# Layer 1's gate stored ready-made, its norm bias moved into the gate step, and the final norm done in one product, in a one-core hybrid decoder trunk

## The chip, the cores and the metric

The kernel is one program on 1 core of one Trainium2 chip. The metric is the device time of one execution in microseconds (us), as the median of the runs; lower is better. Next to it stands one profiled execution, whose trace gives the rows below. Engines are named as the profile names them: PE (TensorE; PEld is its weight load), DVE (VectorE), ACT (ScalarE), POOL (GpSimd), SP (SyncE, which here only issues transfers). ACT and POOL issue some transfers too.

## What is computed

A trunk of two residual layers on 2048 tokens of width 1024, all in float32. Cut to what matters here:

```
# layer 0: retention heads (A) and stick-breaking attention (B), each gated
mixed = concat([o_a * silu(ga), o_b * silu(gb)]);  h = h + mixed @ w_out
h = h + sigmoid(h @ ple_gate) * (p @ ple_proj)          # after every layer

# layer 1: RWKV-7 mixing; r, k, v, g are four projections of the normed h
y = head_norm(recurrence(r, w, k, v, kk, a)) * lnx_g + lnx_b
bonus = sum(r * k * r_k) * v                              # per head
h = h + ((y + bonus) * silu(g)) @ w_out
h = h + sigmoid(h @ ple_gate) * (p @ ple_proj)
out = h * rsqrt(mean(h * h) + eps) * final_gain           # the final norm
```

## The kernel before

Tokens go in two halves of 1024 (`w` = 0, 1), each in two blocks of 512 (`TB`); channels lie on the 128 partitions, in eight blocks (`NB`). Each float32 matrix product is made of three products of a high and a low part (`mm3`, L239 to L241), and `split` (L199 on ACT, L200 on DVE or POOL) makes these parts. The stages in their order:

- half 0: retention and stick-breaking attention, then `tail(0, 0)` (output projection, per-layer embedding), then `l1_proj` (layer 1's projections and the preparation of the recurrence);
- half 1: the same attention, then **the first merge**: the recurrence of layer 1 for half 0 (`recur`, 16 chunks of 64 tokens) runs beside the layer-0 tail of half 1 (`tail_lean`); then `l1_proj` for half 1;
- **the second merge**: the recurrence for half 1 beside three blocks of layer 1's tail (`tail_lean` with l = 1: both blocks of half 0, the first of half 1);
- the final tail: `tail(1, 1)` for the last block, and beside it `finish`, which writes the normed output of the three earlier blocks.

`merge` weaves two generators by planned costs, and a scheduler then sets each engine's order from its own planned timeline. On the chip every engine works its list strictly in that order. Tiles come from pools with a fixed number of buffers, and whoever wants a buffer waits until its last user is done.

The places that the change touches:

- `g_proj` (L1231) projects the gate in groups of two channel blocks. `to_dram` (L1105) empties each of the four accumulators of a group: ACT copies it into a tile `ev` (two buffers, L1108) and ACT issues the store (L1109).
- `gated` (L858) loads a block of the recurrence's result (`stage`) and the gate (`g`), and makes stage·g·sigmoid(g): DVE L866, ACT L867, DVE L868. The final tail has its own form: ACT Silu L713, DVE L714.
- in `block`, the new residual is `o` (DVE L941, two buffers); ACT squares it (L946), for l = 1 DVE multiplies it by the final gain (L949), and SP stores it (L950). The final tail does that on ACT (L779).
- `post` (L1589) norms a chunk: POOL multiplies the value tile `vt` by the bonus (L1603) and `y` by the gain (L1604), DVE adds the bias to `vt` (L1605) and `vt` to `y` (L1607). Gain, bias and bonus are loaded by SP at the head of each recurrence (L1647, L1648).

Of the kernel before, what the change touches and what calls it, by code (L numbers as in the profile page):

```python
# [9 lines left out]
F32 = mybir.dt.float32  # L10
# [3 lines left out]
AF = mybir.ActivationFunctionType  # L14
# [58 lines left out]
C_N = C_HX + 4 * P  # L73


V_G0, V_G1, V_GF, V_MU, V_W0, V_A0, V_KK, V_KA, V_RK, V_GN = 0, 1, 2, 3, 9, 10, 11, 12, 13, 14
V_N = 15


def constants():  # L80
# [54 lines left out]
class Trunk:  # L135
# [44 lines left out]
    def load_vectors(self):  # L180
        nc = self.nc
        v = self.cst.tile([P, V_N * NB], F32, name="vec")
        nc.scalar.dma_start(v, self.i["vec"])
        self.vec = v

        self.omu = self.cst.tile([P, 6 * NB], F32, name="omu")
        nc.vector.tensor_scalar(self.omu, v[:, V_MU * NB : (V_MU + 6) * NB], -1.0, 1.0, op0=ALU.mult, op1=ALU.add)
        self.oka, self.hka = [self.cst.tile([P, NB], F32, name=n) for n in ("oka", "hka")]
        ka = v[:, V_KA * NB : (V_KA + 1) * NB]
        nc.vector.tensor_scalar(self.oka, ka, -0.5, 1.0, op0=ALU.mult, op1=ALU.add)  # L190
        nc.vector.tensor_scalar_mul(self.hka, ka, 0.5)

    def col(self, which, b):
        return self.vec[:, which * NB + b : which * NB + b + 1]
# [491 lines left out]
    def tail(self, l, w, mixed, gates, resid, side=None, ts=range(NTB)):  # L686
# [3 lines left out]
        with ExitStack() as es:  # L690
# [13 lines left out]
            for t in ts:  # L704
                for d in range(NB):
                    sl = slice(t * TB, (t + 1) * TB)
                    gated = gates(d, sl) is not None
                    m = sm.tile([P, TB], F32, tag="m" if gated or d % 2 else "g", name=self.u("m"), bufs=3 if gated or d % 2 else 2)
                    nc.sync.dma_start(m, mixed(d, sl))
                    if gated:  # L710
                        g = sm.tile([P, TB], F32, tag="g", name=self.u("g"))
                        nc.sync.dma_start(g, gates(d, sl))
                        nc.scalar.activation(g, g, AF.Silu)  # L713
                        nc.vector.tensor_tensor(m, m, g, op=ALU.mult)  # L714
                    self.split(m, mx[d][0][:, tok(t)], mx[d][1][:, tok(t)], nc.vector if (d * NTB + t) % 3 < 2 else nc.gpsimd)
            hs = [tuple(hp.tile([P, n], F32R, tag="hp", name=self.u("hp")) for _ in range(2)) for _ in range(NB)]

# [34 lines left out]
            def ple_evac(ob):  # L752
                wq = wqs[ob]

                def evac(t, ps):
                    sl = slice(t * TB, (t + 1) * TB)
                    g = sm.tile([P, TB], F32, tag="g", name=self.u("g"))
                    nc.scalar.activation(g, ps, AF.Sigmoid)
                    q = pp.tile([P, TB], F32, tag="pp", name=self.u("pp"))
                    for d in range(2):  # L760
                        self.mm3(
                            q, (wq[0][:, d], wq[1][:, d]), (pT[d][0][:, tok(t)], pT[d][1][:, tok(t)]), d == 0, d == 1
                        )
                    nc.vector.tensor_tensor(g, g, q, op=ALU.mult)
                    o = sb.tile([P, TB], F32, tag="o", name=self.u("o"))
                    nc.gpsimd.tensor_tensor(
                        o, hs[ob][0][:, tok(t)].bitcast(F32), hs[ob][1][:, tok(t)].bitcast(F32), op=ALU.add
                    )
                    nc.vector.tensor_tensor(o, o, g, op=ALU.add)
                    if ob == 0:  # L770
                        nc.scalar.activation(self.ssacc[:, sl], o, AF.Square)
                    else:
                        nc.scalar.activation(g, o, AF.Square)
                        eng = nc.vector if ob == NB - 1 else nc.gpsimd
                        eng.tensor_tensor(self.ssacc[:, sl], self.ssacc[:, sl], g, op=ALU.add)
                    if l == 0:
                        nc.sync.dma_start(h1[ob][:, sl], o)
                    else:
                        nc.scalar.activation(h1[ob], o, AF.Copy, scale=self.col(V_GF, ob))  # L779

                return evac

# [10 lines left out]
            for t in ts:  # L793
                rbp = self.rows_of(rs[:, (t - ts[0]) * 4 : (t - ts[0]) * 4 + 4], pt)
                for ob in range(NB):
                    o = sb.tile([P, TB], F32, tag="fo", name=self.u("fo"), bufs=8)
                    nc.vector.tensor_tensor(o, rbp, h1[ob][:, tok(t)], op=ALU.mult)
                    (nc.scalar if ob % 2 else nc.sync).dma_start(self.out_at(w, ob, t), o)

    def out_at(self, w, ob, t):  # L800
# [11 lines left out]
    def finish(self, w, h, rs, ts, sb, pt):  # L812
# [11 lines left out]
        for n, (t, ob) in enumerate(units):  # L824
# [2 lines left out]
            if ob == 0:  # L827
                rbp = self.rows_of(rs[:, t * 4 : t * 4 + 4], pt)
            o = sb.tile([P, TB], F32, tag="o", name=self.u("fo"))
            nc.vector.tensor_tensor(o, rbp, xs.pop(0), op=ALU.mult)  # L830
            nc.sync.dma_start(self.out_at(w, ob, t), o)
            yield

    def tail_lean(self, es, parts):
# [23 lines left out]
        def gated(blk, d, tags="g"):  # L858
# [4 lines left out]
            if gates(d, tok(b)) is not None:  # L863
                g = T(tags[d % len(tags)], 2)
                nc.sync.dma_start(g, gates(d, tok(b)))
                nc.vector.tensor_tensor(m, m, g, op=ALU.mult)  # L866
                nc.scalar.activation(g, g, AF.Sigmoid)  # L867
                nc.vector.tensor_tensor(m, m, g, op=ALU.mult)  # L868
            return m

        def spread(staged):
# [8 lines left out]
        def block(blk, staged, following):  # L880
# [33 lines left out]
            for ob in range(NB):  # L914
# [30 lines left out]
                else:  # L945
                    nc.scalar.activation(g, o, AF.Square)  # L946
                    nc.gpsimd.tensor_tensor(self.ssacc[:, sl], self.ssacc[:, sl], g, op=ALU.add)
                if l == 1:
                    nc.vector.tensor_scalar_mul(o, o, self.col(V_GF, ob))  # L949
                nc.sync.dma_start(h1[:, ob, sl], o)  # L950
                yield
            return ahead
# [42 lines left out]
    def l1_proj(self, w, h1):  # L995
# [10 lines left out]
        with ExitStack() as es:  # L1006
# [207 lines left out]
            def v_proj():  # L1214
                xs = mix(2)
                for nh in range(2):
# [12 lines left out]

                    yield from self.proj_N(ws, xs, evac, pj)  # L1230

            def g_proj():
                yield from self.proj_pairs(load(3), mix(3), lambda ob: to_dram(d_g[ob]), pj)

            bnp = pst.tile([P, TB], F32, tag="pt", name=self.u("bnp"))

# [101 lines left out]
    def recur(self, w, es, lean=False, early=0):  # L1338
# [20 lines left out]
        lnx = []  # L1359
        for nm in ("rwkv_lnx_gain", "rwkv_lnx_bias"):  # L1360
            t = fin.tile([P, NB, C], F32, name=self.u("lnx"), bufs=1)
            lnx.append((t, i[nm][0].rearrange("(o s c) -> s o c", s=2, c=C)))
# [225 lines left out]
        def post(s):  # L1588
# [12 lines left out]
            nc.gpsimd.tensor_tensor(y, y, bc(rs), op=ALU.mult)  # L1601
            yield
            nc.gpsimd.tensor_tensor(vt, vt, bc(bonus[:, s]), op=ALU.mult)  # L1603
            nc.gpsimd.tensor_tensor(y, y, lnx[0][0], op=ALU.mult)  # L1604
            nc.vector.tensor_tensor(vt, vt, lnx[1][0], op=ALU.add)  # L1605
            yield
            nc.vector.tensor_tensor(y, y, vt, op=ALU.add)  # L1607
            yield
# [13 lines left out]
        def main():  # L1622
# [19 lines left out]
                yield PRE[1]  # L1642
            for _ in inv(0):
                yield PRE[2]
            for par in range(2):
                for t, src in lnx:
                    nc.sync.dma_start(t[half(par)], src[par].unsqueeze(0).to_broadcast([C, NB, C]))  # L1647
                nc.sync.dma_start(bonus[half(par)], self.d_b[par].rearrange("(c t) o -> t c o", t=C))  # L1648
            b = None
            for s in range(NCH):  # L1650
                self.ready = max(0, s - 1) * C
# [119 lines left out]
def chain(makers):  # L1771
# [18 lines left out]

_INS = [
    "x", "ple_proj", "ple_gate", "even_w_in", "even_w_out", "odd_w_in", "odd_w_out", "rwkv_w1", "rwkv_w2",
    "rwkv_a1", "rwkv_a2", "rwkv_lnx_gain", "rwkv_lnx_bias",
]


def vectors(inputs):
# [3 lines left out]
    for v, x in (  # L1801
# [5 lines left out]
        (V_KK, a("rwkv_k_k", 0)),  # L1807
        (V_KA, a("rwkv_k_a", 0)),
        (V_RK, a("rwkv_r_k", 0)),
    ):  # L1810
        rows[v : v + len(x)] = x
    rows[V_GN, :RH] = np.asarray(inputs["ret_gn_gain"])[0].reshape(RH, P)
# [28 lines left out]
```

## Time and profile before

| | |
|---|---|
| median of 3 runs | 3716.74 us (3715.48 to 3717.23) |
| profiled execution: its own time | 3711.4 us |
| profiled execution: span of the trace | 3709.6 us |
| busy: PE / DVE / ACT / POOL | 91% / 54% / 37% / 26% of the span |
| mean granted PE clock | 0.939 of full speed |

The busy shares are means over stages with different limits. PE's is near the full span, but it holds stretches at a lower granted clock and stretches with gaps. What a change is worth is read from the stage in which it lies, and there from who is waited for.

### The profile page before, as it was taken

How to read it: one execution, taken by the hardware profiler on the slowest of the kernel's cores; microseconds unless marked ns; L12 is line 12 of the kernel's file. 1: busy time of each engine (PE TensorE's matmuls, PEld its weight loads, DVE VectorE, ACT ScalarE, POOL GpSimd, SP SyncE). 2: the span in 40 equal slices, each digit the busy share in tenths (PEclk: the TensorE clock that was granted, in tenths of full speed). 3: DMA queues.
4: the chain of work that ended last, by engine and by line, in shares of the span. 5: the costliest groups of instructions: out<-in, count | busy, mean ns of one | idle time of the engine just before them, and what ended most of it. 6: DMA issues, size and time to landing. Idle time of an engine off the chain costs nothing.

```text
span 3709.6 us, 65403 instructions
## 1 busy us (share of the span) xinstructions
PE 3383.3 (91%) x25640; PEld 2694.0 (73%) x25640; DVE 1991.4 (54%) x3959; ACT 1375.3 (37%) x2671; POOL 971.0 (26%) x1019
## 2 busy tenths in 40 slices
PE   7999999899999999999879998699988698978968
PEld 6888878787666788888767776587656577767756
DVE  3435552452665333567856666641574477566543
ACT  4333442354564222445523333343453143223222
POOL 3345554300000222556512222200000243222322
PEclk9999999899999999999989998699999788979979
DMA  7259765655688216537367655333676777656485
GB/s 263 96 171 271 218 195 177 216 164 182 201 266 288 99 67 194 175 101 148 68 203 210 194 177 144 104 121 138 200 249 178 186 222 211 186 144 183 158 281 197
DMA packets 570788, 671.94 MB, mean 181 GB/s; under 512 B 215408, under 2 KB 416368, under 8 KB 539504
## 3 DMA queue, kind: packets, MB, share of 16 engines
q1 hardware_dynamic: 495072, 578.41, 50.2%
q0 software_dynamic: 40576, 33.56, 4.4%
q10 hardware_dynamic: 34832, 55.78, 4.1%
q8 instruction: 203, 3.33, 0.4%
q14 instruction: 105, 0.86, 0.1%
HBM read 419.50 MB, written 248.12 MB: 180 GB/s over the span
## 4 chain that ended last, share of the span: by engine, by line
PE 71%; DMA 10%; DVE 9%; ACT 3%; SPq 3%; issue 3%; POOL 1%; DVEq 0%; ACTq 0%; POOLq 0%
PE pj L239 17%; PE pj L240 17%; PE pj L241 17%; PE g L1396 2%; PE tp L654 1%; DMA nb<-nad 1%; DVE wb L1450 1%; DVE prd L1444 1%; PE lora L1266 1%; SPq L1429 1%; PE u L1516 1%; PE x L1538 1%; DMA xr<-ar 1%; PE z L625 1%; PE ot L240 1%
## 5 line engine op out<-in xcount | busy, mean ns | idle before, releaser
L239 PE MATMUL pj<-act,w 128*128 128x512 f32 x1216 | 498.5, 414 | 27.0 <-ACT act L199 10.5
L241 PE MATMUL pj<-act,w 128*128 128x512 f32 x1216 | 497.9, 410 | 6.0 <-POOL w L200 5.9
L240 PE MATMUL pj<-act,w 128*128 128x512 f32 x1216 | 496.9, 409 | 2.5 <-DVE act L200 1.7
L239 PE MATMUL pj<-xs,w 128*128 128x512 f32 x768 | 296.8, 401 | 21.0 <-ACT xs L199 9.5
L240 PE MATMUL pj<-xs,w 128*128 128x512 f32 x768 | 305.7, 399 | 6.3 <-DVE xs L200 6.2
L241 PE MATMUL pj<-xs,w 128*128 128x512 f32 x768 | 301.5, 395 | 0.0
L239 PEld LDWEIGHTS pj<-act,w 128*128 128x128 f32 x1216 | 238.3, 197 | 83.7 <-ACT act L199 13.1
L241 PEld LDWEIGHTS pj<-act,w 128*128 128x128 f32 x1216 | 238.4, 196 | 60.4 <-POOL w L200 9.0
L240 PEld LDWEIGHTS pj<-act,w 128*128 128x128 f32 x1216 | 238.9, 196 | 54.3 <-DVE act L200 3.0
L239 PE MATMUL pj<-w,act 128*128 128x512 f32 x640 | 257.7, 407 | 19.3 <-ACT w L199 9.8
L240 PE MATMUL pj<-w,act 128*128 128x512 f32 x640 | 256.7, 401 | 2.9 <-POOL w L200 2.9
L241 PE MATMUL pj<-w,act 128*128 128x512 f32 x640 | 254.3, 401 | 0.0
L636 DVE TENSOR_TENSOR_SCAN rr<-om,rr,ones 128x512 f32<-128x512 f32 (+3 forms) x160 | 202.0, 1274 | 46.8 <-ACT om L630 39.2
L645 POOL TENSOR_TENSOR be<-be,rr 128x512 f32<-128x512 f32 (+3 forms) x160 | 176.7, 1107 | 164.4 <-DVE rr L636 82.3
L200 POOL TENSOR_TENSOR w<-wraw,w 128x1024 fp32r<-128x1024 f32 x72 | 162.1, 2253 | 204.1 <-ACT w L199 198.1
L239 PEld LDWEIGHTS pj<-xs,w 128*128 128x128 f32 x768 | 145.4, 190 | 70.3 <-issue 14.5
L240 PEld LDWEIGHTS pj<-xs,w 128*128 128x128 f32 x768 | 145.9, 190 | 43.9 <-DVE xs L200 13.0
L241 PEld LDWEIGHTS pj<-xs,w 128*128 128x128 f32 x768 | 145.9, 190 | 33.9 <-issue 2.7
L1396 PE MATMUL g<-xr,kb 64*128 64x128 f32 x1024 | 116.8, 311 | 52.0 <-DVE grb L1421 23.0
L199 ACT CAST w<-wraw 128x1024 fp32r<-128x1024 f32 x105 | 104.6, 1000 | 144.7 <-DMA wraw<-in_even_w_in 38.7
L239 PEld LDWEIGHTS pj<-w,act 128*128 128x128 f32 x640 | 122.3, 192 | 48.4 <-ACT sg L448 12.1
L458 POOL TENSOR_SCALAR tst<-gs 128x128 f32<-128x128 f32 x64 | 34.4, 538 | 468.8 <-DMA gs<-gstate 246.5
(330 smaller groups left out, 7511.5 us busy)
## 6 DMA issues: line engine op xcount, KB each, us to landing
w<-parts SPq DMA_DIRECT2D x145, 1024.0 KB, 6.0
parts<-w SPq DMA_DIRECT2D x97, 1024.0 KB, 5.5
wraw<-in_odd_w_in SPq DMA_DIRECT2D x32, 512.0 KB, 7.2
ar<-ar SPq DMA_DIRECT2D x32, 512.0 KB, 4.4
w<-v SPq DMA_DIRECT2D x128, 128.0 KB, 3.8
xr<-ar SPq DMA_DIRECT2D x64, 256.0 KB, 5.5
kb<-kb SPq DMA_DIRECT2D x32, 512.0 KB, 5.1
kg<-dk POOLq DMA_DIRECT2D x24, 512.0 KB, 5.0
```

Source lines behind the costliest of these rows:

```text
L199: nc.scalar.copy(hi, src)
L200: (lo_eng or nc.vector).tensor_tensor(lo, src, hi.bitcast(F32), op=ALU.subtract)
L239: nc.tensor.matmul(ps, a[0], b[0], start=first, stop=False)
L240: nc.tensor.matmul(ps, a[0], b[1], start=False, stop=False)
L241: nc.tensor.matmul(ps, a[1], b[0], start=False, stop=last)
L625: nc.tensor.matmul(z[:, :kw], q[:, 1, qc], kt[:, 0, :kw], start=False, stop=True)
L636: nc.vector.tensor_tensor_scan(rr[:, 0:kw][:, ::-1], om[:, ::-1], self.ones.to_broadcast([P, kw]), rr[:, kw : kw + 1], op0=ALU.mult, op1=A ...
L645: nc.gpsimd.tensor_tensor(be, be, rr[:, 1 : kw + 1], op=ALU.mult)
L654: nc.tensor.transpose(tp[:, j], wt[qi][:, j * P : (j + 1) * P], self.ident)
L1266: nc.tensor.matmul(pss[j], w2[jw][hs, oc], mid[jm][hs, sl], start=n == 0, stop=n == 2)
L1396: nc.tensor.matmul(ps[:, j], kb[br, ob], xr[br, par, ob], start=True, stop=True)
L1429: nc.sync.dma_start(nad[b].rearrange("u r t -> r u t"), na[b * 16 : (b + 1) * 16, :, o : o + 16])
```

## The change

Layer 1's gate is stored as z·(1 + tanh(z/2)), which is twice silu(z): the accumulator is now emptied by a Tanh on ACT and one product on DVE that reads the accumulator again, and ACT's store waits for DVE. The factor one half goes to the gain and the bonus (two small scalings on ACT at the head of each recurrence) and to the bias. The bias is no longer added in `post`; it becomes a per-channel column (`hlb`) that is added in the same DVE instruction that multiplies by the gate, so `gated` and the final tail need one DVE instruction and no ACT instruction for layer 1. The final gain is no longer multiplied into the stored residual, but enters the last product, which multiplies by gain and row factor in one DVE instruction. In the final tail the residual is written straight into the tile that is kept.

```diff
+        nc.vector.tensor_scalar_mul(self.hlb, v[:, V_LB * NB : (V_LB + 1) * NB], 0.5)
...
                         nc.sync.dma_start(g, gates(d, sl))
-                        nc.scalar.activation(g, g, AF.Silu)
-                        nc.vector.tensor_tensor(m, m, g, op=ALU.mult)
+                        if l == 0:
+                            nc.scalar.activation(g, g, AF.Silu)
+                            nc.vector.tensor_tensor(m, m, g, op=ALU.mult)
+                        else:
+                            nc.vector.scalar_tensor_tensor(
+                                m, m, self.hlb[:, d : d + 1], g, op0=ALU.add, op1=ALU.mult
+                            )
...
-                    o = sb.tile([P, TB], F32, tag="o", name=self.u("o"))
+                    o = h1[ob] if l else sb.tile([P, TB], F32, tag="o", name=self.u("o"))
...
-                    else:
-                        nc.scalar.activation(h1[ob], o, AF.Copy, scale=self.col(V_GF, ob))
...
-                    nc.vector.tensor_tensor(o, rbp, h1[ob][:, tok(t)], op=ALU.mult)
+                    nc.vector.scalar_tensor_tensor(
+                        o, h1[ob][:, tok(t)], self.col(V_GF, ob), rbp, op0=ALU.mult, op1=ALU.mult
+                    )
...
-            nc.vector.tensor_tensor(o, rbp, xs.pop(0), op=ALU.mult)
+            nc.vector.scalar_tensor_tensor(o, xs.pop(0), self.col(V_GF, ob), rbp, op0=ALU.mult, op1=ALU.mult)
...
-                nc.vector.tensor_tensor(m, m, g, op=ALU.mult)
-                nc.scalar.activation(g, g, AF.Sigmoid)
-                nc.vector.tensor_tensor(m, m, g, op=ALU.mult)
+                if l == 0:
...
+                else:
+                    nc.vector.scalar_tensor_tensor(m, m, self.hlb[:, d : d + 1], g, op0=ALU.add, op1=ALU.mult)
...
-                if l == 1:
-                    nc.vector.tensor_scalar_mul(o, o, self.col(V_GF, ob))
                 nc.sync.dma_start(h1[:, ob, sl], o)
...
+            def twice_silu(dst):
+                def evac(t, ps):
+                    e = ev.tile([P, TB], F32, tag="ev", name=self.u("ev"), bufs=2)
+                    nc.scalar.activation(e, ps, AF.Tanh, scale=0.5)
+                    nc.vector.scalar_tensor_tensor(e, e, 1.0, ps, op0=ALU.add, op1=ALU.mult)
+                    nc.scalar.dma_start(dst[:, t * TB : (t + 1) * TB], e)
...
-            nc.gpsimd.tensor_tensor(y, y, lnx[0][0], op=ALU.mult)
-            nc.vector.tensor_tensor(vt, vt, lnx[1][0], op=ALU.add)
+            nc.gpsimd.tensor_tensor(y, y, lnx, op=ALU.mult)
...
-                for t, src in lnx:
-                    nc.sync.dma_start(t[half(par)], src[par].unsqueeze(0).to_broadcast([C, NB, C]))
+                nc.sync.dma_start(lnx[half(par)], gain[par].unsqueeze(0).to_broadcast([C, NB, C]))
...
+            nc.scalar.activation(lnx, lnx, AF.Copy, scale=0.5)
+            nc.scalar.activation(bonus, bonus, AF.Copy, scale=0.5)
```

Three places show how the order moves. All lie where half 1's `l1_proj` hands over to the second merge. Line numbers of the changed kernel are 2 to 17 higher: its L202, L1432, L1435 and L1436 are the L200, L1417, L1420 and L1421 of before.

First DVE, at the first chunks of the second merge (`g` are the chunks' score products from PE, `xr` and `grb` what DVE makes of them). Before:

```order
L1417 TENSOR_TENSOR xr_26647<-g_26753,k 64x512
L1417 TENSOR_TENSOR xr_26647<-g_26754,k 64x512
L1421 TENSOR_TENSOR grb_26752<-g_26753,k 64x256
L1421 TENSOR_TENSOR grb_26752<-g_26754,k 64x256
L1605 TENSOR_TENSOR vt_27819<-vt_27819,lnx_26510 128x512
L1417 TENSOR_TENSOR xr_26647<-g_26802,k 64x512
L1417 TENSOR_TENSOR xr_26647<-g_26803,k 64x512
```

and now:

```order
L1432 TENSOR_TENSOR xr_26647<-g_26753,k 64x512
L1432 TENSOR_TENSOR xr_26647<-g_26754,k 64x512
L1436 TENSOR_TENSOR grb_26752<-g_26753,k 64x256
L1436 TENSOR_TENSOR grb_26752<-g_26754,k 64x256
L1432 TENSOR_TENSOR xr_26647<-g_26802,k 64x512
L1432 TENSOR_TENSOR xr_26647<-g_26803,k 64x512
```

The bias addition between two chunk groups is gone, and the second group follows the first directly.

Second ACT, at the same place (`na` is ACT's copy of the score products, `w` a weight part that it casts, `lnx` and `bon` the gain and the bonus). Before:

```order
L1420 ACTIVATE na_26658<-g_26700 64x4x64
L1540 COPY xs_27506<-x_27489 128x512
L1420 ACTIVATE na_26658<-g_26753 64x4x64
L1420 ACTIVATE na_26658<-g_26754 64x4x64
L1420 ACTIVATE na_26658<-g_26802 64x4x64
L1420 ACTIVATE na_26658<-g_26803 64x4x64
L199 CAST w_26678<-wraw_26679 128x1024
```

and now:

```order
L1435 ACTIVATE na_26658<-g_26700 64x4x64
L1663 ACTIVATE lnx_26526<-lnx_26526 128x512
L1664 ACTIVATE bon_26527<-bon_26527 128x128
L1555 COPY xs_27498<-x_27481 128x512
L1435 ACTIVATE na_26658<-g_26753 64x4x64
L1435 ACTIVATE na_26658<-g_26754 64x4x64
L201 CAST w_26678<-wraw_26679 128x1024
L1435 ACTIVATE na_26658<-g_26802 64x4x64
L1435 ACTIVATE na_26658<-g_26803 64x4x64
```

The two scalings stand ahead of three copies of the recurrence, and the cast of the weight part now stands ahead of the second group's two `na` copies, behind which it stood before.

Third DVE, a little earlier, at the last accumulators of the gate projection (`act` and `pT` are low parts for the first block of the tail). Before:

```order
L200 TENSOR_TENSOR pT_26827<-g_26776,pT_26826 128x512
L200 TENSOR_TENSOR act_26608<-stage_26547,act_26607 128x512
L200 TENSOR_TENSOR act_26612<-stage_26554,act_26611 128x512
L200 TENSOR_TENSOR act_26616<-stage_26561,act_26615 128x512
L200 TENSOR_TENSOR act_26620<-stage_26568,act_26619 128x512
```

and now:

```order
L202 TENSOR_TENSOR pT_26827<-g_26776,pT_26826 128x512
L202 TENSOR_TENSOR act_26608<-stage_26561,act_26607 128x512
L1244 SCALAR_TENSOR_TENSOR ev_26475<-ev_26475,pj_26290 128x512
L1244 SCALAR_TENSOR_TENSOR ev_26479<-ev_26479,pj_26291 128x512
L202 TENSOR_TENSOR act_26612<-stage_26566,act_26611 128x512
L202 TENSOR_TENSOR act_26616<-stage_26571,act_26615 128x512
L202 TENSOR_TENSOR act_26620<-stage_26576,act_26619 128x512
```

The last two of the 32 new products stand between the low parts that the tail's first output product reads.

## Rows read from the trace of the kernel before

**Rows 1.** The page: the chain that ended last, by engine.

```profile
PE 71%; DMA 10%; DVE 9%; ACT 3%; SPq 3%; issue 3%; POOL 1%; DVEq 0%; ACTq 0%; POOLq 0%
```

**Rows 2.** Windows: gate projection, half 0 and half 1; second merge; final tail.

```profile
core 0: us, PE busy (x) PEld busy (x) DVE busy (x) ACT busy (x) POOL busy (x), PEclk, DMA share, GB/s
1065.00:1206.00 141.00, 135.77 (x554) 96.99 (x553) 90.95 (x155) 79.50 (x141) 0.00 (x0) 0.98 0.83 283
...
2560.00:2855.00 295.00, 271.59 (x1074) 183.98 (x1072) 163.01 (x238) 141.31 (x244) 3.71 (x4) 0.96 0.61 198
2855.00:3577.00 722.00, 615.54 (x7678) 487.91 (x7678) 442.52 (x1021) 209.29 (x412) 204.21 (x149) 0.85 0.65 191
3577.00:3710.00 133.00, 108.74 (x448) 84.86 (x448) 47.78 (x79) 30.53 (x49) 30.73 (x24) 0.90 0.66 229
```

**Rows 3.** Groups of DVE's instructions in the second merge (2855 to 3577).

```profile
L949 DVE TENSOR_SCALAR o<-o,vec 128x512 f32<-128x512 f32 x24 | 22.4, 931 | 6.3 <-ACT g L946 4.7 <-ACT ssacc L944 1.4
...
L866 DVE TENSOR_TENSOR stage<-stage,g 128x512 f32<-128x512 f32 x16 | 16.3, 1017 | 18.4 <-DMA g<-g 13.6 <-DMA stage<-yT 4.8
...
L868 DVE TENSOR_TENSOR stage<-stage,g 128x512 f32<-128x512 f32 x16 | 14.9, 930 | 5.4 <-ACT g L867 5.3
L1605 DVE TENSOR_TENSOR vt<-vt,lnx 128x512 f32<-128x512 f32 x16 | 13.7, 858 | 36.9 <-POOL vt L1603 36.8
```

**Rows 4.** The chain: by line from 3000 to 3120, then single pieces.

```profile
by line: DMA wraw<-in_ple_gate 11.8%; issue 6.0%; DMA g<-g 5.1%; DVE wb L1450 4.7%; DVE prd L1444 4.5%; DVE stage L866 4.3%; PE pj L241 4.2%; DVE stage L868 3.9%; POOL w L200 3.3%; DMA kb<-kb 3.2%; PE pj L239 3.0%; PE pj L240 2.9%; DVE o L9
...
3000.95 1.28 ACT L867
...
3048.20 1.43 DVE o L949
...
3546.01 1.62 DVE o L949
```

**Rows 5.** Timeline at the second merge's start: DVE, PE, ACT, SP.

```profile
2888.61 0.69 DVE L1605 TENSOR_TENSOR vt<-vt,lnx 128x512 f32<-128x512 f32 x1 [14.81 <-POOL vt L1603]
...
2891.12 2.61 PE L1396 MATMUL g<-xr,kb 64*128 64x128 f32 x16 [15.30 <-DVE grb L1421]
...
2892.23 1.04 ACT L199 CAST w<-wraw 128x1024 fp32r<-128x1024 f32 x1 [1.07 <-DMA wraw<-in_odd_w_out]
...
2874.49 0.63 SPq L1647 DMA_DIRECT2D lnx<-in_rwkv_lnx_bias  x1
2875.17 0.63 SPq L1648 DMA_DIRECT2D bon<-b  x1
```

**Rows 6.** The bias addition's group in the first merge (1857 to 2313).

```profile
L1605 DVE TENSOR_TENSOR vt<-vt,lnx 128x512 f32<-128x512 f32 x12 | 13.2, 1098 | 17.3 <-POOL vt L1603 17.3
```

**Rows 7.** Groups in the gate projection: half 0, and last a wait in half 1.

```profile
L1108 ACT COPY ev<-pj 128x512 f32<-128x512 f32 x16 | 9.3, 583 | 16.5 <-PE pj L241 9.9 <-DMA g<-ev 4.6 <-DMA r<-r 1.5
...
L1300 DVE SCALAR_TENSOR_TENSOR r<-kp,vec,r 128x512 f32<-128x512 f32 x8 | 6.0, 747 | 0.0
L1294 DVE SCALAR_TENSOR_TENSOR k<-k,vec,rnp 128x512 f32<-128x512 f32 x8 | 6.0, 746 | 0.4
...
L1269 ACT ACTIVATE sg<-lora,w0h 128x512 f32<-128x512 f32 x7 | 4.8, 686 | 16.9 <-DVE kb L1303 9.8 <-PE lora L1266 5.2 <-DVE rs L341 1.8
...
L1280 DVE TENSOR_TENSOR_SCAN L<-scan,sg 128x512 f32<-128x512 f32 x16 | 19.6, 1225 | 47.6 <-ACT sg L1273 47.6
```

**Rows 8.** Timeline of PE in half 1's projection and at its end.

```profile
2745.42 1.64 PE L1266 MATMUL lora<-mid,w 64*128 64x512 f32 x3 [3.91 <-ACT sg L1269]
...
2853.39 0.69 PE L239 MATMUL pj<-act,w 128*128 128x512 f32 x1 [2.18 <-ACT ev L1108]
```

**Rows 9.** Timeline of one gate step of eight at the final tail's start.

```profile
3594.22 0.32 SPq L712 DMA_DIRECT2D g<-g  x1
...
3595.48 0.63 ACT L713 ACTIVATE g<-g 128x512 f32<-128x512 f32 x1 [0.63 <-DMA g<-g]
...
3596.14 0.69 DVE L714 TENSOR_TENSOR m<-m,g 128x512 f32<-128x512 f32 x1 [0.57 <-ACT g L713]
...
3596.86 0.32 SPq L712 DMA_DIRECT2D g<-g  x1
```

More of the change, by code (lines that the diff above doesn't have):

```diff
@@ L73 @@
 C_N = C_HX + 4 * P
-V_G0, V_G1, V_GF, V_MU, V_W0, V_A0, V_KK, V_KA, V_RK, V_GN = 0, 1, 2, 3, 9, 10, 11, 12, 13, 14
-V_N = 15
+V_G0, V_G1, V_GF, V_MU, V_W0, V_A0, V_KK, V_KA, V_RK, V_GN, V_LB = 0, 1, 2, 3, 9, 10, 11, 12, 13, 14, 15
+V_N = 16
 def constants():
@@ L191, in load_vectors @@
         nc.vector.tensor_scalar_mul(self.hka, ka, 0.5)
+        self.hlb = self.cst.tile([P, NB], F32, name="hlb")
+        nc.vector.tensor_scalar_mul(self.hlb, v[:, V_LB * NB : (V_LB + 1) * NB], 0.5)
     def col(self, which, b):
@@ L865, in gated @@
                 nc.sync.dma_start(g, gates(d, tok(b)))
-                nc.vector.tensor_tensor(m, m, g, op=ALU.mult)
-                nc.scalar.activation(g, g, AF.Sigmoid)
-                nc.vector.tensor_tensor(m, m, g, op=ALU.mult)
+                if l == 0:
+                    nc.vector.tensor_tensor(m, m, g, op=ALU.mult)
+                    nc.scalar.activation(g, g, AF.Sigmoid)
+                    nc.vector.tensor_tensor(m, m, g, op=ALU.mult)
+                else:
+                    nc.vector.scalar_tensor_tensor(m, m, self.hlb[:, d : d + 1], g, op0=ALU.add, op1=ALU.mult)
             return m
@@ L1230, in v_proj @@
                     yield from self.proj_N(ws, xs, evac, pj)
+            def twice_silu(dst):
[4 more added lines that the diff above has]
+                    nc.scalar.dma_start(dst[:, t * TB : (t + 1) * TB], e)
+                return evac
             def g_proj():
-                yield from self.proj_pairs(load(3), mix(3), lambda ob: to_dram(d_g[ob]), pj)
+                yield from self.proj_pairs(load(3), mix(3), lambda ob: twice_silu(d_g[ob]), pj)
             bnp = pst.tile([P, TB], F32, tag="pt", name=self.u("bnp"))
@@ L1357, in recur @@
         TF = lambda tag, shape, bufs: fin.tile(shape, F32, tag=tag, name=self.u(tag), bufs=bufs)
[L1359 to L1362, printed above, removed]
+        lnx = fin.tile([P, NB, C], F32, name=self.u("lnx"), bufs=1)
         bonus = fin.tile([P, NCH, NB], F32, name=self.u("bon"), bufs=1)
@@ L1644, in main @@
                 yield PRE[2]
+            gain = i["rwkv_lnx_gain"][0].rearrange("(o s c) -> s o c", s=2, c=C)
             for par in range(2):
-                for t, src in lnx:
-                    nc.sync.dma_start(t[half(par)], src[par].unsqueeze(0).to_broadcast([C, NB, C]))
+                nc.sync.dma_start(lnx[half(par)], gain[par].unsqueeze(0).to_broadcast([C, NB, C]))
                 nc.sync.dma_start(bonus[half(par)], self.d_b[par].rearrange("(c t) o -> t c o", t=C))
+            nc.scalar.activation(lnx, lnx, AF.Copy, scale=0.5)
+            nc.scalar.activation(bonus, bonus, AF.Copy, scale=0.5)
             b = None
@@ L1792 @@
     "x", "ple_proj", "ple_gate", "even_w_in", "even_w_out", "odd_w_in", "odd_w_out", "rwkv_w1", "rwkv_w2",
-    "rwkv_a1", "rwkv_a2", "rwkv_lnx_gain", "rwkv_lnx_bias",
+    "rwkv_a1", "rwkv_a2", "rwkv_lnx_gain",
 ]
@@ L1809, in vectors @@
         (V_RK, a("rwkv_r_k", 0)),
+        (V_LB, a("rwkv_lnx_bias", 0)),
     ):
```

## The prediction

> **What bounds the kernel now.** I read first the page's chain that ended last: 71% of it is PE, 10% transfers, 9% DVE [rows 1]. So work taken off DVE or ACT is worth something only where PE waits for it, and I read by stage. In the gate projections PE is the bound: busy 135.8 of 141 us in half 0 and 271.6 of 295 us in half 1, with DVE at 91 and 163 us [rows 2]. The reader is to see that DVE has room there, and PE none. The second merge is different: of 722 us PE is busy 615.5 at a granted clock of 0.85, so 106 us are gaps and part of the busy time runs at the lower level; DVE is busy 442.5 us, ACT and POOL under 30% [rows 2]. There the recurrence's chain passes from engine to engine, and a wait on any of them can hold PE. The final tail has 24 us of gaps in 133 [rows 2].
>
> In the second merge I then read DVE's groups and the chain. The three groups that the change removes or thins are L949 with 22.4 us, L866 with L868 at 31.2 us, and L1605 with 13.7 us of work and 36.9 us of waiting for POOL [rows 3]. Of these the chain holds only a part: from 3000 to 3120, L866 is 4.3% and L868 3.9% of 120 us (5.2 and 4.7 us), and beside them stands the load of the gate with 5.1% (6.1 us) [rows 4].
>
> The sum is made against the profiled execution's own 3711.4 us, which is 5.3 us under the median of the runs; the result is carried to the median by adding the same 5.3.
>
> **The change, part by part.**
>
> *Start of the second merge: -1 us.* Before, DVE stood 14.8 us at L1605, behind POOL's product that waited for its values, and PE stood 15.3 us behind DVE [rows 5]. The order of the changed kernel has no L1605 there, so this stall cannot come back in that place. But it has two others on ACT: the scalings wait for gain and bonus, whose last transfer was issued at 2875.17 [rows 5], and the cast of a weight part now stands ahead of the second group's `na`. That cast could start only at 2892.23, when its weights had landed [rows 5]; `na` then comes at about 2893, where before PE went on at 2891. The transfers ahead of these weights lose two bias loads of 0.63 us each [rows 5], about 1.3 us. So I expect the same stall under another name, and 1 us gained. Bounds: -11 (all but a few us of the 15.3) and +3 (the weights no earlier, and the two copies behind the cast).
>
> *Gate step, residual scaling, bias addition in the second merge: -10 us.* On DVE, 24 L949 go (22.4 us), 16 pairs at 1.02 and 0.93 us become 16 single instructions, and 16 L1605 go [rows 3]. A scalar_tensor_tensor takes 0.75 us against 0.69 for a plain product outside the merge [rows 7, 9]; in the merge I scale it with L866's mean, to 1.1 us, so the pairs save 31.2 - 17.6 = 13.6 us. All of it is 49.7 us less DVE work, 11% of 442.5. On the chain I count four pieces of L949 (the first 1.43, the last 1.62 us [rows 4], about 6 together), L868's 4.7 us, one table load for the sigmoid of 1.28 us [rows 4], and 1 us for L1605: 13 us. What is late next stands beside them: the gate's load, which the new instruction waits for as L866 did, and the weights' loads with 11.8% [rows 4]. So I keep three quarters, 10 us. Bounds: nothing, if the loads and PE fill every place, and -30 (below).
>
> *First merge: -2 us.* Twelve additions of 1.10 us and 17.3 us of waiting go from DVE [rows 6]; two bias loads go from SP; two ACT scalings come. In the second merge about 1 of 14 us of this group was on the chain, so 13.2 us give 1, and I add 1 for the loads. Bounds -8 and +2.
>
> *Gate projection: +1, -1 and +2 us.* Each of 32 accumulators was emptied by an ACT copy of 0.583 us; now it takes a Tanh, which with two operands per partition takes 0.686 us, and a DVE product that reads the accumulator, 0.75 us [rows 7]. It is free about 0.85 us later plus the wait in DVE's queue, and the store on ACT's queue waits for DVE, with ACT's next work behind it. DVE gets 12.0 us in each half, to 103 of 141 us in half 0 [rows 2]: PE's stream covers it, since the next group's accumulators are needed one after the other. If that cover is gone, it costs what DVE's queue costs (the slow rival). I take +1 for the stragglers. In half 1 the first eight gate steps lie inside this stage: PE stood 3.91 us for a sigmoid-like ACT step [rows 8] behind them; two products of 0.69 us less ahead of it give -1. At the hand-over PE's first product of the tail already waited 2.18 us for the last copies [rows 8]; now there are two more DVE products between the low parts, and the accumulator is freed by DVE after a Tanh that itself waits for the tile's store. I take +2. Bounds of the three together: 0 and +24.
>
> A PSUM read on DVE costs nothing more by the rows: L1294, which reads `rnp` from there, takes 746 ns, L1300, without one, 747 ns [rows 7]. [...]
>
> *Final tail: -3 us, end +0.5.* At its start one gate step of eight takes 2.64 us, from one load's issue to the next: landing, 0.63 us Silu, 0.69 us product [rows 9]. Without the Silu and its hand-over (0.66) and with 0.75 for 0.69 it is 2.04, but PE's products for a block need about 2.1, so 0.54 us for each of six steps that follow at this pace: 3 us. Bounds -4.2 (seven steps at 0.6) and 0. The last eight products at the end are 0.06 us longer each: +0.5. The eight ACT copies of the residual (L779) lie behind the squares that the norm needs, and cost nothing now; `finish` (24 products, 0.06 us more each) is covered by PE.
>
> Sum: -1 - 10 - 2 + 1 - 1 + 2 - 3 + 0.5 = -13.5 us. That is 3697.9 for the profiled execution and 3703 us for the median.
>
> **Rivals.**
>
> *The merges give nothing back (same).* For it: PE, loads and weight parts hold most of the chain [rows 1, 4]. Against it: the 106 us of gaps and a clock of 0.85 say that PE waits a lot there [rows 2]. Without the 10 and the 2, and all else as above, the sum is -1.5: 3715 us.
>
> *PE waits for the new product (slower).* PE needs a group's accumulators back at four places in each half, the hand-over among them: eight. DVE works in order, and its scan L1280 alone waited 47.6 us in 16 times, 3.0 us each [rows 7]. If the new products stand behind such waits so that PE is 3.0 us late at each of the eight, it is 24 us in place of my 3: -13.5 + 21 = +7.5, 3724 us. It is slower from a mean of 2.1 us at each place, and measurably from 3.0. Against it: PE's idle time in the gate projection of half 0 was 5 us in all [rows 2], and the tiles' stores already delay copies without PE noticing.
>
> *DVE's relief shortens the second merge by more (faster still).* DVE's work and its wait at L1605 are 442.5 + 36.9 us there; 22.4 + 13.6 + 13.7 + 36.9 = 86.6 us of that go [rows 2, 3]. If a third of it comes out, it is 29 in place of 10: -32.5, 3684 us. For it: L949 takes up to 1.62 us [rows 4] against its mean of 0.93, and L866 1.02 us [rows 3] where the same product takes 0.69 outside [rows 9], so the engines hinder each other there. [...]
>
> **How the numbers follow.** My forecast 0.45 (its own range 3693 to 3710), the larger gain 0.15, nothing from the merges 0.23, the slow case 0.17. The likeliest gives the time, 3703 us. The range goes down to 3675, where half of the 86.6 us would nearly come out, and up to 3725, the slow case at 3.0 us. A measurement here tells about 0.2% (7.4 us) from no change. Of the forecast a twentieth falls within that: faster 0.58, same 0.25, slower 0.17.
>
> **What would show it.** In the profile after: no DVE wait for POOL at the start of the second merge, but an ACT wait for the weights ahead of `na`, and PE still idle there for some 15 us; the second merge shorter by about 11 us, DVE under 400 us busy in it; gate projections within 2 us of before, with no PE wait for DVE `ev` over 2 us but the one at the hand-over; gate steps at the final tail's start about 2.1 us apart. I am wrong if PE waits for `ev` in many places, or if the second merge's order, planned anew, puts other waits on the recurrence's chain; that plan is the part that I cannot price from the trace.

## The result, and the profile after

The changed kernel takes 3693.4 us (median, 3690.6 to 3699.3) against 3716.8 of before: ratio 0.9934, 95% interval 0.992 to 0.9948, 23 us less. The profiled execution's own time is 3690.6 us, its span 3688.5. It stands beside that of before (3711.4, 3709.6) as the medians do, so its rows can be compared.

The windows that answer to [rows 2] (gate projection of half 0, second merge, final tail; columns as there), with the stages' borders where they now lie:

```profile
1067.90:1213.00 145.10, 135.38 (x558) 96.71 (x556) 100.16 (x171) 80.49 (x140) 0.00 (x0) 0.98 0.82 281
...
2856.00:3545.00 689.00, 601.23 (x7679) 474.65 (x7678) 394.76 (x958) 199.93 (x395) 194.74 (x148) 0.90 0.67 195
3545.00:3688.50 143.50, 111.60 (x448) 88.45 (x448) 52.03 (x84) 20.99 (x34) 31.04 (x24) 0.86 0.67 232
```

The second merge is 33 us shorter (722 to 689): DVE is down by 48 us, PE's gaps went from 106 to 88 us, and its busy time by 14 us at a granted clock of 0.90 in place of 0.85. The final tail is 10 us longer. So the total near the forecast is made of two larger numbers than I had.

At the second merge's start the stall is there under another name, as forecast. Timeline of PE and of ACT (what ended the idle time stands in brackets):

```profile
2855.22 0.77 PE L241 MATMUL pj<-act,w 128*128 128x512 f32 x1 [5.28 <-DVE ev L1244]
...
2877.02 2.53 PE L1411 MATMUL g<-xr,kb 64*128 64x128 f32 x16 [4.48 <-DVE grb L1436]
...
2888.30 0.79 PE L241 MATMUL pj<-act,w 128*128 128x512 f32 x1 [8.75 <-ACT w L201]
...
2887.21 1.04 ACT L201 CAST w<-wraw 128x1024 fp32r<-128x1024 f32 x1 [10.29 <-DMA wraw<-in_odd_w_out]
```

PE no longer stands 15.3 us behind DVE [rows 5]; it stands 4.5 and 8.8 us, the second behind the cast that waits for its weights. All its waits from 2846 to 2960 come to 31.6 us against 33.1. The first of them is the hand-over, where it waits 5.28 us for the new product in place of 2.18 [rows 8]; so the waits behind it are 26.3 us against 30.9.

The new instructions, in the gate projection of half 0 (L1243, L1244; L1319 is an old one of the same form, without an accumulator) and in the second merge (L878):

```profile
L1243 ACT ACTIVATE ev<-pj 128x512 f32<-128x512 f32 x16 | 9.5, 592 | 11.9 <-DMA g<-ev 5.5 <-DMA r<-r 3.6 <-PE pj L243 2.5
...
L1244 DVE SCALAR_TENSOR_TENSOR ev<-ev,pj 128x512 f32<-128x512 f32 x16 | 10.9, 684 | 5.8 <-ACT ev L1243 3.0 <-DMA x<-in_xT 2.7
...
L1319 DVE SCALAR_TENSOR_TENSOR a<-a,k 128x512 f32<-128x512 f32 x8 | 5.5, 685 | 0.0
...
L878 DVE SCALAR_TENSOR_TENSOR stage<-stage,hlb,g 128x512 f32<-128x512 f32 x16 | 15.9, 993 | 18.6 <-DMA g<-g 15.9 <-DMA stage<-yT 2.6
```

The Tanh takes 0.592 us (I had 0.686), the product from PSUM 0.684 (0.75), and the single gate step 0.99 (1.1). It waits as long for its load as L866 did, 15.9 us against 13.6 [rows 3].

### The profile page after: what moved, and what is told of

It is laid out like the page before. It is cut to its first block, busy times and chain, and to the rows that moved or that the text cites. A ratio compares the mean times of both kernels' runs of the same rounds, so it can differ in the third digit from the quotient of the medians.

```text
span 3688.5 us, 65344 instructions
## 1 busy us (share of the span) xinstructions
PE 3370.6 (91%) x25640; PEld 2685.8 (73%) x25640; DVE 1940.9 (53%) x3912; ACT 1345.9 (36%) x2629; POOL 962.2 (26%) x1019
## 5 line engine op out<-in xcount | busy, mean ns | idle before, releaser
L202 POOL TENSOR_TENSOR w<-wraw,w 128x1024 fp32r<-128x1024 f32 x72 | 160.2, 2228 | 445.5 <-ACT w L201 427.9
L242 PEld LDWEIGHTS pj<-xs,w 128*128 128x128 f32 x768 | 146.5, 191 | 42.2 <-DVE xs L202 10.3
L241 PEld LDWEIGHTS pj<-w,act 128*128 128x128 f32 x640 | 122.4, 192 | 53.1 <-ACT sg L450 15.2
## 6 DMA issues: line engine op xcount, KB each, us to landing
wraw<-in_odd_w_in SPq DMA_DIRECT2D x32, 512.0 KB, 7.5
ar<-ar SPq DMA_DIRECT2D x32, 512.0 KB, 4.6
kb<-kb SPq DMA_DIRECT2D x32, 512.0 KB, 6.4
kg<-dk POOLq DMA_DIRECT2D x24, 512.0 KB, 5.0
```

The source lines that it names most:

```text
L202: (lo_eng or nc.vector).tensor_tensor(lo, src, hi.bitcast(F32), op=ALU.subtract)
L241: nc.tensor.matmul(ps, a[0], b[0], start=first, stop=False)
L242: nc.tensor.matmul(ps, a[0], b[1], start=False, stop=False)
```

## The experiments

Each kernel was timed in five rounds against before on the same chip; the ratio and its interval are from these. Over the 29 executions of before in the last of these rounds its median is 3714.2 us; against that the changed kernel's 3693.4 is 21 us, so the gain is known as 21 to 23 us. "Second merge" is the time from the last store of the gate to the last transposes (721.0 us before, 686.9 changed; in the changed orders the last two stores follow one another, and it is the first of the two, 0.6 us earlier), "tail" from there to the end of the span (134.8, 146.5), both in the one profiled execution. One execution is not exact: e4 has the changed kernel's order up to its last transposes, and its second merge is 11.7 us longer.

| run | ratio to before | second merge, tail (us) |
|---|---|---|
| the changed kernel | 0.9934 (0.992 to 0.9948) | 686.9, 146.5 |
| e1: gain alone | 0.9996 (0.998 to 1.0012) | 713.8, 142.1 |
| e2: all but the gain | 0.9922 (0.9904 to 0.994) | 689.3, 142.3 |
| e3: bias back in `post` | 0.9962 (0.9949 to 0.9976) | 691.0, 141.0 |
| e4: five buffers in `finish` | 0.993 (0.9911 to 0.995) | 698.6, 144.8 |
| e5: e2, gate step in two DVE instructions | 1.0001 (0.999 to 1.0013) | 721.0, 136.3 |
| e6: e2, Sigmoid kept | 0.9945 (0.9931 to 0.9958) | 693.1, 142.2 |
| e7: bias alone | 0.9928 (0.991 to 0.9947) | 691.7, 140.4 |
| e8: e2 with five buffers | 0.9935 (0.9918 to 0.9951) | 687.3, 145.0 |
| e9: before, RATIO_B 0.98 | 0.998 (0.9969 to 0.9992) | 706.0, 144.7 |
| e10: before, RATIO_B 0.92 | 0.9992 (0.998 to 1.0004) | 703.8, 144.4 |
| e11: changed, RATIO_B 0.96 | 0.9948 (0.9934 to 0.9961) | 698.9, 144.1 |
| e12: changed, RATIO_B 0.90 | 0.9996 (0.9981 to 1.0011) | 698.0, 155.6 |

**The parts one by one.** e1 makes only the edits on the final gain in the kernel before; e2 takes just these back in the changed kernel.

```diff
-                if l == 1:
-                    nc.vector.tensor_scalar_mul(o, o, self.col(V_GF, ob))
                 nc.sync.dma_start(h1[:, ob, sl], o)
...
-            nc.vector.tensor_tensor(o, rbp, xs.pop(0), op=ALU.mult)
+            nc.vector.scalar_tensor_tensor(o, xs.pop(0), self.col(V_GF, ob), rbp, op0=ALU.mult, op1=ALU.mult)
```

> Of the change only the final gain is moved (the 24 products L949 and the eight ACT copies of the final tail go, the last product multiplies by gain and row factor); gate and bias stay as before. Theory A (the second merge gives back DVE work in proportion: 33 us for 49.7 us removed, of which L949 is 22.4): the second merge is 15 us shorter, the final tail gives 5 back, 3707 us. Theory B (the gain is the order planned anew, not the work): no such share; the time is within 4 us of before (3717) or takes nearly all of the gain (3695). My prediction's own size (10 us for all of the work): 3712.

> The changed kernel with the final gain put back into the stored residual (L949 and the ACT copies again); gate and bias as changed. Theory A: of 49.7 us of DVE work 27.3 go, the second merge is 18 us shorter than before, the first 3, the final tail gives 4 to 8 back: 3702 us. Theory B: no proportion; 3693 (all of the gain) or 3717 (none). A sum of this run's gain and that of the gain alone far from 24 us speaks for B.

e1 came out at no change and e2 at the whole gain. The 24 products L949, 22.4 of the 49.7 us of DVE work, were worth nothing that can be measured: the profile has the merge 7 us shorter and the tail 7 us longer. Two more pairs that differ by the same edit say the same, e2 and the changed kernel (0.9922, 0.9934) and e8 and e4 (0.9935, 0.993). The proportion of theory A is refuted: of its sums for e1 and e2 only the sign of e2 held. The two gains add up to 30 us against the 23 of both edits together; that is no clear sign by itself.

e3 puts the bias back (the gate step is then `tensor_tensor(m, m, g)`):

```diff
             nc.gpsimd.tensor_tensor(y, y, lnx, op=ALU.mult)
+            nc.vector.tensor_tensor(vt, vt, lnb, op=ALU.add)
...
+                nc.sync.dma_start(lnb[half(par)], bias[par].unsqueeze(0).to_broadcast([C, NB, C]))
+            nc.scalar.activation(lnb, lnb, AF.Copy, scale=0.5)
```

> The changed kernel with the bias added to the value tile again (L1605, 32 DVE additions, its two loads at the head of each recurrence, a third ACT scaling); the gate step is a plain product. Theory A: 13.7 us of DVE work come back in the second merge, 13.2 in the first: 9 and 2 us, 3704 us. Prediction's size: 1 us in each merge, 3695. Theory C (what stalls is DVE's wait for POOL at L1605, 36.9 us before): DVE waits some 30 us there again and the second merge is 15 us or more longer, 3708.

It lost 10 of the 23 us (0.9962 against 0.9934). In total this is what theory A had (3704 us; the ratio gives 3703), but not from where theory A took it. DVE's group of this addition, in the first merge of before and of e3, and in e3's second merge:

```profile
L1605 DVE TENSOR_TENSOR vt<-vt,lnx 128x512 f32<-128x512 f32 x15 | 15.2, 1015 | 20.4 <-POOL vt L1603 20.3
...
L1617 DVE TENSOR_TENSOR vt<-vt,lnb 128x512 f32<-128x512 f32 x15 | 11.8, 789 | 36.5 <-POOL vt L1615 33.8 <-DMA stage<-mx 2.7
...
L1617 DVE TENSOR_TENSOR vt<-vt,lnb 128x512 f32<-128x512 f32 x16 | 16.1, 1007 | 33.8 <-POOL vt L1615 33.8
```

The wait of theory C is back in full in the second merge, 33.8 us, and that merge is not longer for it (691.0 against 686.9 and 698.6, the two executions of the changed kernel's order). What is longer is the first merge: 531.5 us, one execution, against 518.0 in the mean of six executions with the changed order (512.0 to 524.8). Before it is 529.8 in the mean of four, with 16 us less of this wait than in e3, so the time did not follow the wait's length there either. Theory C's wait came back, and its price did not.

e7 is the counterpart, the bias alone moved, with Sigmoid, second product and the stored gate as before:

```diff
-                nc.vector.tensor_tensor(m, m, g, op=ALU.mult)
+                    nc.vector.scalar_tensor_tensor(m, m, self.col(V_LB, d), g, op0=ALU.add, op1=ALU.mult)
                 nc.scalar.activation(g, g, AF.Sigmoid)
                 nc.vector.tensor_tensor(m, m, g, op=ALU.mult)
...
-            nc.vector.tensor_tensor(vt, vt, lnx[1][0], op=ALU.add)
```

> Before, with the bias alone moved: the first product of the gate step adds it in the same instruction, L1605 and its two loads go, Sigmoid and second product stay, the gate is stored as before. My prediction's size (1 us in each merge): ratio 0.999. From the run with the bias back in `post` (0.9962 against 0.9934 of the changed kernel): 0.997, 3703 us, most of it in the first merge, where the wait of 17 us goes. Rival (DVE's wait at L1605 only moves elsewhere, as its total of 260 to 282 us in every kernel says): 1.000.

It reached 0.9928, the whole gain, with the smallest edit; every expectation was too small. The total of DVE's waits did stay, as the rival says (256 us from the last gate store to the last copy of `y`, 256 to 294 over the fourteen kernels), and the time fell all the same. Its first merge took 508.5 us. It is one order, so the 23 us are not the bias alone for certain. A Sigmoid step with 18 table loads, as before, did not keep it from that.

**What in the gate step is worth something.** Both start from e2; e5 splits the one DVE instruction (the first piece below), e6 puts an ACT step ahead of it (the second).

```diff
-                    nc.vector.scalar_tensor_tensor(m, m, self.hlb[:, d : d + 1], g, op0=ALU.add, op1=ALU.mult)
+                    nc.vector.tensor_scalar_add(m, m, self.hlb[:, d : d + 1])
+                    nc.vector.tensor_tensor(m, m, g, op=ALU.mult)
...
+                    nc.scalar.activation(g, g, AF.Sigmoid)
                     nc.vector.scalar_tensor_tensor(m, m, self.hlb[:, d : d + 1], g, op0=ALU.add, op1=ALU.mult)
```

> The kernel of the run 'gate only' (ratio to before 0.992, second merge 689 us against 720 before), whose 24 gate steps of the merges' layer-1 blocks are done in two DVE instructions (the bias added, then the product), with no ACT step between, as there. DVE has again as many instructions per gate step as before. Theory W (the gate's part of the gain is DVE's work): the merge gets some 14 us of work back and half or more of its 30 us, ratio 0.997 or more, 3702 us. Theory T (it is the ACT step between the two products, its table load and its two hand-overs): no change against 'gate only', ratio 0.992, 3683 us. Theory B (any new order may do it): no saying, either.

> The kernel of 'gate only' with an ACT Sigmoid on the loaded gate ahead of the one DVE instruction in the 24 gate steps of the merges (the gate is then not the reference's; the final tail has none). Theory W: no change against 'gate only', 0.992, 3683 us. Theory T: the table loads of the Sigmoid (18 in all before, 12 in the changed kernel, 1.28 us each) and the hand-over come back ahead of the recurrence's ACT work; the merge is 10 to 25 us longer, ratio 0.996 to 0.999, 3698 to 3710 us.

e6 lost less than theory T asks (3690 us against 3683, the intervals overlap). It is no full test of T: four table loads came back in half 1's projections, but its second merge holds one, as e2's and that of before do until its last steps. e5 alone would be a victory for theory W: the whole gain gone with 24 DVE instructions. But beside e7 it can't be. The second merge of e5 and then of e7, with the same DVE work:

```profile
2860.00:3581.00 721.00, 614.16 (x7676) 481.63 (x7675) 423.08 (x1004) 199.04 (x394) 197.74 (x148) 0.89 0.66 190
...
2840.00:3532.00 692.00, 592.07 (x7661) 469.02 (x7660) 422.00 (x984) 207.41 (x410) 201.43 (x148) 0.89 0.68 195
```

DVE is busy 423 and 422 us, ACT even longer in e7, and e7 is 29 us shorter, more than the 11.7 us by which one order spread. The amount of DVE's work does not set this time.

**The order alone.** Any edit there lets the planner set a new order for all that follows. So in the last four kernels nothing is edited but the weight by which the second merge's two generators are woven:

```diff
-RATIO_B = 0.95
+RATIO_B = 0.98
```

> Before, not an instruction added or taken away: only the weight by which `merge` weaves the second merge's two generators (RATIO_B) is 0.98 in place of 0.95, so that the order is another from some 2860 us on. Theory W (work taken off DVE and ACT makes the gain): ratio 1.000, within 0.2%. Theory B (the order does): a change by up to 25 us, either way. Theory Q (a finer B: the kernels with 469 dense products on PE's list behind the last chunk's state product, before, gain only and two-step gate, are the slow ones, those with 439 or 498 the fast): here 439 are left, ratio 0.993 to 0.995.

> As the last, with RATIO_B 0.92; 493 dense products are left behind the last chunk's state product. Theory W: 1.000. Theory B: a change by up to 25 us. Theory Q: 0.992 to 0.995.

> The changed kernel with RATIO_B 0.96 alone; 469 dense products are left behind the last chunk's state product, as in the slow kernels. Theory W: 0.9934 as the changed kernel. Theory B: up to 25 us off it. Theory Q: 0.998 to 1.001, nearly the whole gain is gone though all the work is still out.

> The changed kernel with RATIO_B 0.90 alone; 500 dense products are left. Theory W: 0.9934. Theory Q: 0.992 to 0.994. It is also the try at a version that beats both kernels: below 0.990 it would, beyond the interval.

e12 lost the whole gain, with every instruction of the change in place; e11 lost 5 us, e9 won 7 on before, e10 nothing that can be told. Theory B holds: one work in three orders differs by up to 23 us (21 by the medians). Theory Q falls: e11 with 469 products is fast, e12 with 500 and e10 with 493 are slow. e12 in the second merge, to be read beside the changed kernel's row above:

```profile
2857.00:3555.00 698.00, 605.54 (x7655) 478.55 (x7653) 398.97 (x941) 197.51 (x393) 194.70 (x147) 0.88 0.65 190
```

Of the 20 us between these two executions 11 lie here and 9 in the tail. The 11 are no more than what one order spread here (e4, 698.6 us), so they are not shown to be the new order's. The tail of 155.6 us is the longest of all kernels, and there PE's first product comes 20.7 us after the last transposes (14.0 in the changed kernel).

**The final tail.** e4 and e8 give `finish` five output buffers, in the changed kernel and in e2:

```diff
-            o = sb.tile([P, TB], F32, tag="o", name=self.u("fo"))
+            o = sb.tile([P, TB], F32, tag="o", name=self.u("fo"), bufs=5)
```

> The changed kernel, with five buffers in place of two for the output tile of `finish`, which runs beside the final tail. Theory D (the final tail lost its gain because DVE and SP's queue stand behind stores of this tile that wait for a free buffer: first product 13.9 us after the last transposes against 10.0 before): the wait goes to 10 us or less, the final tail from 143.5 to some 135 us, 3685 us. Rival E (the loads for the gate step stand behind the stores in SP's queue, whatever the buffers): 13 us again, 3693. Rival F (the final tail is bound by PE's lower clock alone): no change of its 143 us.

> The kernel of 'gate only' with five buffers for the output tile of `finish`. If the stores' buffers hold the entry of the final tail there too (15.7 us from the last transposes to the first product): 4 to 6 us less than 'gate only', ratio 0.9905, 3678 us. If not (five buffers in the changed kernel: 13.1 us in place of 13.9, the time 0.993 against 0.9934): 0.992, 3683 us.

Neither is faster. The tail of the changed kernel (DVE, PE), then of e4 (DVE, PE):

```profile
3592.85 0.75 DVE L837 SCALAR_TENSOR_TENSOR fo<-fx,vec,rbp 128x512 f32<-128x512 f32 x1 [10.66 <-DMA out<-fo]
...
3555.98 1.22 PE L241 MATMUL pj<-act,w 128*128 128x512 f32 x2 [12.84 <-ACT act L201]
...
3594.89 0.79 PE L241 MATMUL pj<-act,w 128*128 128x512 f32 x1 [4.15 <-DVE r L730]
```

```profile
3605.49 0.75 DVE L837 SCALAR_TENSOR_TENSOR fo<-fx,vec,rbp 128x512 f32<-128x512 f32 x1 [9.58 <-DMA fx<-h]
...
3568.35 1.22 PE L241 MATMUL pj<-act,w 128*128 128x512 f32 x2 [12.06 <-ACT act L201]
```

With two buffers `finish` waits for its stores, with five for its loads, 10.7 against 9.6 us at the same place, and PE's entry wait stays (12.8, 12.1). Theory D falls. In DVE's list of the changed kernel the sum L730 comes next behind that product of `finish`; it starts at 3594.14, and PE waits 4.15 us for it. That loads and stores hold each other in SP's queue (theory E) fits; it was not tested by itself. No version here beats the changed kernel beyond the intervals.

## Why the prediction was right, and where its steps were not

The time, the sign and the forecast's size held: 3693 where I said 3703, at the edge of the forecast's own range. The parts did not, and that their sum came near is in part luck: the two merges together gave 2.3 times what I had for them, other stages took part of that back, and the same edits in the order of e12 take 3714 us, where my rival "nothing from the merges" stood. Up to the second merge all kernels with before's order there (before, e1, e9, e10) have one list of instructions, and all with the changed one (changed, e2, e4, e8, e11, e12) another, so each stage can be taken from four and from six executions. The means of the stages' lengths, between the starts of the same instructions (the first column sum of `ssacc`, the first `lora` product, the bonus's transpose, the first copy of `y`, the last normed `hn`, the last store of the gate, the last transposes `yt`):

| stage | before's lists | changed lists | difference | I had |
|---|---|---|---|---|
| to layer 1's projections, half 0 | 712.0 | 714.4 | +2.4 | 0 |
| its first part, to the first decay product | 229.0 | 231.2 | +2.2 | 0 |
| to the end of the gate projection, half 0 | 260.0 | 262.9 | +2.9 | +1 |
| attention of half 1 | 656.9 | 654.9 | -2.0 | 0 |
| first merge | 529.8 (523.8 to 536.5) | 518.0 (512.0 to 524.8) | -11.8 | -2 |
| projections of half 1, hand-over | 473.3 | 472.4 | -0.9 | +1 |
| second merge (lists differ) | 711.1 (703.8 to 721.0) | 693.2 (686.9 to 698.9) | -17.9 | -11 |
| tail (lists differ) | 141.5 | 146.4 | +4.9 | -2.5 |
| all | 3713.6 | 3693.4 | -20.2 | -13.5 |

- **First merge: mis-sized, -12 in place of -2, beyond its bound of -8.** The step that failed is "In the second merge about 1 of 14 us of this group was on the chain, so 13.2 us give 1". I priced the addition by its own pieces on one chain, and in the wrong merge (my window also ended at 2313; to 2381 the profile has 15 additions, 15.2 us, with 20.4 us of waits). That it is the bias is likely, from four orders of this merge: with the addition in `post` 529.8 (mean of before's list) and 531.5 us (e3, one execution), without it 518.0 and 508.5 (e7, one execution); e5 and e6, with the changed list there, took 519.8 and 521.9. It is not proven: each of these edits also set a new order, from early in the kernel on, and this merge's own weight (RATIO) was never varied alone. That DVE's standing behind POOL was the cost is not shown either, since e3 has more of it than before at the same length.
- **Second merge: -18 in the mean, and no sum over its work.** "So I keep three quarters, 10 us" supposed that a share of the removed pieces on the chain comes out. e1 removes the four pieces of L949 (about 6 us on the chain) and gains nothing. They did run slower beside POOL: in before the three L949 that ran while POOL did nothing took 0.48 us, the other 21 took 0.49 to 1.61, a mean of 1.00. What slows them there was not tested by itself, and taking them out shortened nothing that can be measured. The table load of 1.28 us did not go: it stands at 2998 for the next Sigmoid (L944), where before it stood at 3001 for L867. e5 and e7 have equal DVE work and differ by 29 us there. e12 has all the work out and gains nothing in the end, though its second merge (698.0 us) is shorter than any of before's lists. Those lie at 703.8 to 721.0 us, the changed ones at 686.9 to 698.9: some gain comes with the edits here, but e3, e5 and e7 give no one edit the credit. The start was right in kind: behind the hand-over PE waits 26.3 us against 30.9, -4.6 for -1, inside its bounds. My last sentence, that the plan is the part which I cannot price, was the one to weigh: it is as large as the gain.
- **An estimate of what is left when orders are averaged.** Six runs with the gate and bias edits in one order or another (changed, e2, e4, e8, e11, e12) have a mean ratio of 0.9944; four without them (before, e1, e9, e10) 0.9992: some 18 us for the edits, while single orders lie from 8 us under that mean to 19 above it. (e5 is left out because it splits the gate step; with it the mean is 0.9952 and the edits' share 15 us.) In the profiles the first merge holds 12 of the gain, second merge and tail 13, and the other stages lose 5.
- **Gate projection: +2.9 for +1, hand-over right in kind.** Half 0 is just outside the 2 us that I allowed, but e7, whose gate is emptied as before, took 254.4 us there against 260.0: another order can move this stage by more. PE waited for `ev` over 2 us only at the hand-over, as said; the slow rival (3 us at eight places) did not come. The projections of half 1 with the hand-over gave -0.9 for +1.
- **The PSUM read cost no more here.** The product that reads the accumulator takes 684 ns at 128x512, and L1319, the same form without one, 685 ns. (The 746 and 747 ns of [rows 7] are a form with a column per channel in place of a number; I priced the new product by them, and so too high.)
- **Final tail: wrong sign, +4.9 for -2.5.** The step "Without the Silu and its hand-over (0.66) and with 0.75 for 0.69 it is 2.04" left out what comes next: the loads. From the first block's product to the eighth's it is 21.2 us (3555.98 to 3577.16) where it was 21.7, 0.5 us for the 3 that I had. The step now waits for its loads, 7.2 us in all for `m` and 1.5 for `g`:

```profile
3561.03 1.31 DVE L719 SCALAR_TENSOR_TENSOR m<-m,hlb,g 128x512 f32<-128x512 f32 x1 [1.27 <-DMA m<-yT]
```

  And the entry is later: 14.0 us from the last transposes to the first product, 10.0 before. That goes with the order: e9 and e10, with before's work, have 13.6 and 16.5. The largest part lies behind the eighth block, before and now:

```profile
3606.44:3709.62 103.18, 89.41 (x385) 71.80 (x385) 34.06 (x58) 21.78 (x35) 28.18 (x22) 0.94 0.59 208
...
3577.16:3688.49 111.33, 92.87 (x386) 74.39 (x384) 33.67 (x59) 16.04 (x26) 28.45 (x22) 0.90 0.59 207
```

  PE's gaps there grow by 4.7 us, 4.15 of them the wait behind `finish` shown above, so "`finish` ... is covered by PE" failed too; the other 3.5 us are PE's busy time, at a granted clock of 0.90 in place of 0.94. From the last chunk's `y` to the end it is 162.6 us before and 164.0 now, so what the recurrence's end won (27.7 to 17.5 us) the tail gave back.
- **Not in the sum: the start.** The vector of constants grew from 15 to 16 rows, and the planner issued the loads of the first 40 us in another order. The first row factors come 2.5 us later. PE's product of them starts at 43.91 before and at 43.85 in e3, which has 15 rows; with 16 rows it starts at 46.68 in e7, and in the changed kernel:

```profile
46.44 1.86 PE L377 MATMUL rbp<-k,rs 128*128 128x128 f32 x7 [6.29 <-DVE rs L344]
```

Of the rivals, "DVE's relief shortens the second merge by more" came nearest in the profile (-33 us there, with the tail's +12; in the mean of the orders -18), but not by its cause. What stays open: which feature of an order makes the second merge fast, why the first merge gives back more in e7 than in the changed kernel, and how much of that merge's gain is its own new order. A second load for the bias, to keep the 15 rows, was not tried.

## What to carry to other kernels

Where a planner sets the order anew after each edit, time one work in two or three orders first: a gain smaller than their spread (here up to 23 us) can't be credited to the edit from one order. Take apart a bundle of edits before believing it: here one addition moved out of the recurrence's epilogue was, in the one order tried, worth as much as all. And follow each gain to the end of the kernel: here the second merge was 17.9 us shorter in the mean of the lists and the tail behind it 4.9 us longer, and in the changed kernel's tail the gate step stood 8.7 us in all behind its loads.

## What the runs showed of the hardware beside that

Four executions of one list of instructions (before, e1, e9, e10) differ by 12.7 us in the first merge alone (523.8 to 536.5). The shortest, e9's, and the longest:

```profile
1857.00:2381.00 524.00, 442.33 (x6496) 356.73 (x6496) 333.51 (x809) 152.01 (x311) 124.95 (x104) 0.88 0.60 174
...
1855.50:2381.60 526.10, 445.99 (x6496) 359.56 (x6496) 332.07 (x811) 152.08 (x312) 125.66 (x104) 0.86 0.60 174
...
1857.10:2393.70 536.60, 450.65 (x6496) 363.30 (x6496) 331.50 (x810) 151.76 (x311) 126.22 (x104) 0.86 0.59 170
```

In the longest PE, on the same 6496 products, is busy 8.3 us longer than in the shortest, at a granted clock of 0.86 in place of 0.88, and its gaps grow by 4.3 us, from 81.7 to 86.0 us. But e9 has the lower clock, too, with the smallest gaps of all, 80.1 us: the sum of the gaps does not tell the granted clock here. The second merge spread by 11.7 us in the two executions of the changed kernel's list (686.9, e4's 698.6). A stage of such a merge read from one profile is good to some 10 us.
